# Neighbourhood attention with woven projections: low weight halves by adding DMAs, and low-rank follow-ups queued later

## The chip, the cores and the metric

The kernel runs on one core of a Trainium2 chip. The metric is the device time of one execution in microseconds. A core has a matrix engine (PE, with its weight loads shown as PEld), three elementwise engines (DVE, ACT, POOL), a queue engine that issues most transfers (SP), and 16 DMA engines that move the data. Each engine works through its own instruction queue in order and waits at semaphores for the others.

## The reference, cut to what matters

One layer of a hybrid backbone: a modulated RMS norm, one wide input projection `h @ w_in`, an RWKV branch and a neighbourhood-attention branch side by side, a gated merge, and a feed-forward part. There are 640 tokens (512 latent grid tokens and 128 context tokens), 1024 features, 8 heads of 64 in each branch, all in float32.

```python
h = _rmsnorm(x, p["norm1_g"]) * (1.0 + sc1) + sh1
u_rw, u_na, gate_rw, gate_na = jnp.split(h @ p["w_in"], IN_SPLITS, axis=-1)
o_rw, s_new = _rwkv_branch(u_rw, s0, ...)      # u_rw: r, k, v, and the low-rank inputs wd, ad, gd
q, k, v = jnp.split(u_na, 3, axis=-1)
o_na = _na_latent(q, k, v, ctx_k, ctx_v, p["na_rpb"])
merged = (jax.nn.sigmoid(gate_rw) * (o_rw @ p["w_o_rwkv"])
          + jax.nn.sigmoid(gate_na) * (o_na @ p["w_o_na"]))
x = x + g1 * (merged @ p["w_out"])
```

In the RWKV branch `wd` goes through a tanh and `gd` through a sigmoid before they are multiplied by their second, low-rank matrices (`rw_w_up`, `rw_a_up`, `rw_g_up`); every column of `u_rw` is first mixed with its left and right neighbour in time (`_centred_shift`).

## The kernel before, in words

**Products in halves.** A float32 product of full precision is made of three faster ones: each operand is a high half (a cast to the short form) and a low half (what the cast lost), and PE computes high*high + high*low + low*high. `feat_gen` issues them for one 128-column chunk of weights: 16 matmuls that use the weight's high half `whi`, then 8 that use its low half `wlo`, for the token half 0 to 319, and the same 24 for the tokens 320 to 639. One chunk is thus a **unit** of 48 matmuls.

**Making the halves.** `wdma` (L163) has SP load a chunk of 512 KB into a staging buffer `wst`; there are two such buffers. `wcast` makes the halves, in one of two ways, chosen by one letter of the string `wl` for each unit. With "d": ACT casts `wst` to `whi` (L173) and DVE subtracts, `wlo = wst - whi` (L175). With "p": ACT writes `-wst` in the short form to `wlo` (L171), POOL issues a DMA that adds `wst` to it (L172), and ACT casts `whi` (L173). In the "p" form the staging buffer is free for the next load when the adding DMA has landed, in the "d" form when DVE has subtracted.

**The stage around the change.** Neighbourhood attention runs in 20 blocks (4 pairs of heads, five query blocks each) in the loop over `k` with 22 steps. Step `k` issues `na_o(k-2)` (PE: weighted values; ACT L185 and DVE L186 split the result), `na_l(k)` (PE L899: logits into a PSUM tile `lg` of which there is one; DVE L905 or L912: bias and maximum), `na_t(k-1)` (PE L928: transposes of the probabilities `L` into PSUM tiles `pt`, two of them; ACT L933 copies them out), the exponentials (ACT L909 or L914), 6 woven matmuls, `na_m(k)` (DVE L921: reciprocals; POOL L922: `L` times the reciprocal, two for the two heads), then a bias window for a later block (`window`, POOL L801) and, at step 7 alone, `prep_cast` (ACT L570 casts the second low-rank matrices, POOL L573 makes their low halves), then some 12 more woven matmuls, and at some steps two rounds of the modulation product (`ada_gen`, PE L984, with the loads L965 on SP). From step 10 on the preparation of the first RWKV head pair (`prep_a`, `prep_b`) is interleaved too; its low-rank products (PE L592, L594) borrow the `pt` tiles and ACT L597 or L600 reads them out; its products for the key norm end in DVE L629 and L631.

**The woven units.** The woven matmuls are those of nine units, in the order of `order`: l0 l1 k0 r0 v0 l2 g0 g1 g2 (low-rank inputs, keys, receptances, values, gates). `stream` gives one matmul at a time, loads two units ahead, and queues the cast of unit i+1 when unit i has made 6 matmuls.

**The queue of follow-ups.** `later(fn, cost, more)` appends work with a due time of `off[0] + more` woven matmuls, where `off[0]` is 6 in this stage; the cast of the next unit is appended as due at once. `tick` counts down one per matmul and issues from the head of the list only: what stands behind an entry that isn't due waits for it, even if it is due itself.

```python
    def tick(n):
        for p in pend:
            p[0] -= n
        while pend and pend[0][0] <= (-24 if hold[0] else 0):
            pend.pop(0)[2]()
```

After a unit's last matmul `proj_gen` queues the copy out of PSUM, and the neighbour mixing (`shift`: ACT L521, DVE L522 and L524) in two parts. For the low-rank units `lora_gen` adds a tanh (ACT L711 for l0; L706 and DVE L707 for l2), and for l0 and l1 two calls of `two` that split a result (ACT L701, DVE L702 into `LX`).

**What sets the order.** In this stage `tc.manual_schedule(engines=FIRST)` keeps PE, POOL, DVE and ACT in exactly the order in which the Python code issues. SP isn't among them: its queue is ordered by the planner, which expects times by a model of its own.

Of the kernel before, what the change touches and what calls it, by code (L numbers as in the profile page):

```python
# [7 lines left out]
F32 = mybir.dt.float32  # L8
F32R = mybir.dt.float32r
AF = mybir.ActivationFunctionType  # L10
ALU = mybir.AluOpType
# [59 lines left out]
    h2=0.91, jobs=((2, 9, 28), (2, 9, 28), (2, 9, 28), (2, 11, 28)),  # L71
    mds=((4, 12), (4, 12), (4, 12), (4, 14)), bud=((1.8, 0.8), (1.3, 1.8)), off=6, tk=2, h3=1,
    h4=1.07, g1=2, km="dddddddd", kb="ddpd", ma="d", yo="pppp", r0="pd", rl=(0, 0, 0), lh=(0, 0, 1, 1),
    wl="dddddddddppppppppppppppppppppppppppdpppppppppppp", nu=9, jo=(2, 0, 1), na=(
        "6.0.12.0.1 6.0.12.0.0 6.0.12.0.0 6.0.12.0.2 6.0.12.0.0 6.0.12.0.2 6.0.12.0.0 6.0.12.0.2 6.0.12.0.0 "
        "6.0.12.0.2 6.0.12.1.0 6.1.12.1.2 6.2.12.2.0 6.1.12.2.2 6.0.12.2.0 6.1.12.1.2 6.2.14.2.0 "
        "6.2.14.1.2 6.2.14.2.0 6.2.14.2.0 6.3.18.2.0 10.0.10.0.0"))
# [30 lines left out]
def body(ctx: ExitStack, tc: tile.TileContext, xs, xp, cols, consts, w_ada, b_row, w_rw, w_qkv,  # L108
# [3 lines left out]
    pe, act, dve, pool, sp = nc.tensor, nc.scalar, nc.vector, nc.gpsimd, nc.sync  # L112
# [22 lines left out]
    def nm(s):  # L135
        cn[0] += 1
        return f"{s}_{cn[0]}"
# [28 lines left out]
    def wcast(w, eng=None):  # L166
        st, n, pl, nhl = w
        hi = pl.tile([P, 1024], F32R, tag="whi", bufs=nhl, name=nm("whi"))
        lo = pl.tile([P, 1024], F32R, tag="wlo", bufs=nhl, name=nm("wlo"))
        if eng is pool:  # L170
            act.activation(lo[:, :n], st[:, :n], AF.Copy, scale=-1.0)  # L171
            pool.dma_start(lo[:, :n].bitcast(F32), st[:, :n], accum_op=ALU.add)  # L172
        act.copy(hi[:, :n], st[:, :n])  # L173
        if eng is not pool:
            dve.tensor_tensor(out=lo[:, :n], in0=st[:, :n], in1=hi[:, :n].bitcast(F32), op=ALU.subtract)  # L175
        return hi, lo

    def wload(src, eng=None):
        return wcast(wdma(src), eng)
# [269 lines left out]
    lg_ = kp.tile([P, NT], F32, name="lg_")  # L449
# [28 lines left out]
    def later(fn, cost=(0.5, 0), more=0):  # L478
        if off[0]:
            pend.append([off[0] + more, cost, fn])  # L480
        else:
            fn()
# [21 lines left out]
    def proj_gen(ci, out, ps_, usb, utag, ubufs, w):  # L504
        U = usb.tile([P, 643], F32, tag=utag, bufs=ubufs, name=nm("U"))
        pool.memset(V(U[:, :], [[513, 2]]), 0.0)
        pool.memset(U[:, 642:643], 0.0)
        ps0 = ps_()
        yield from feat_gen(ps0, w, (hh, hl), 8, 0, H2)
        later(lambda: act.copy(U[:, 1:321], ps0[:, :H2]))  # L510
        ps1 = ps_()
        yield from feat_gen(ps1, w, (hh, hl), 8, H2, NT)

        def u_out():
            act.copy(U[:, 321:513], ps1[:, 0:192])
            act.copy(U[:, 514:642], ps1[:, 192:320])

        def shift(a, b, u):
            o = out[:, a:b]
            n = b - a  # L520
            act.activation(o, U[:, u:u + n], AF.Identity, scale=dcol(dm, ci))  # L521
            dve.scalar_tensor_tensor(out=o, in0=U[:, u - 1:u - 1 + n], scalar=col("mu0", ci),  # L522
                                     in1=o, op0=ALU.mult, op1=ALU.add)
            dve.scalar_tensor_tensor(out=o, in0=U[:, u + 1:u + 1 + n], scalar=col("mu1", ci),  # L524
                                     in1=o, op0=ALU.mult, op1=ALU.add)

        later(u_out, (0.6, 0))
        later(lambda: shift(512, 640, 514), (0.4, 0.7), 2)
        later(lambda: shift(0, 512, 1), (0.8, 1.5), 5)
# [163 lines left out]
    gtag = ["fl"]  # L693

    def lora_gen(i, w):

        yield from proj_gen(12 + i, lg_, flps, sb, "U", len(gtag), w)

        def two(d):
            rr, ro = slice(64 * d, 64 * d + 64), slice(64 - 64 * d, 128 - 64 * d)  # L700
            act.copy(LX[i][d][rr, :], lg_[rr, :])  # L701
            dve.tensor_tensor(out=LX[i][d][ro, :], in0=lg_[rr, :], in1=LX[i][d][rr, :].bitcast(F32),  # L702
                              op=ALU.subtract)

        if i == 2:
            later(lambda: act.activation(lg_, lg_, AF.Tanh, scale=0.5), (0.8, 0), 8)  # L706
            later(lambda: dve.tensor_scalar(out=lg_, in0=lg_, scalar1=0.5, scalar2=0.5, op0=ALU.mult, op1=ALU.add),  # L707
                  (0, 0.5), 12)
            return
        if i == 0:  # L710
            later(lambda: act.activation(lg_, lg_, AF.Tanh), (0.8, 0), 8)  # L711
        for d in range(2):
            later(lambda d=d: two(d), (0.8, 0.8), 12 + 6 * d)

    def some(n):
        for _ in range(n):
# [3 lines left out]
    def unit(g, e):  # L720

        i, eng = int(g[1:]), eng_of(e)
        if g[0] in "ab":
            return 24 if g[0] == "a" else 18, lambda: merge_load(g[0], i), \
                lambda wt: merge_cast(*wt, eng), lambda w: merge_gen(g[0], i, w)
        if g[0] == "g":
            return 48, lambda: wdma(w_rw[15 + i]), lambda w: wcast(w, eng), \
                lambda w: gate_gen(i, w, flps, sb, gtag[-1])
        ci, dst = {"k": (4 + i, kt_), "r": (i, rt_), "v": (8 + i, vp0), "l": (12 + i, lg_)}[g[0]]
        return 48, lambda: wdma(w_rw[ci]), lambda w: wcast(w, eng), \  # L730
            lambda w: proj_gen(ci, dst, flps, sb, "U", len(gtag), w) if g[0] != "l" else lora_gen(i, w)
# [48 lines left out]
    with s1:  # L780
# [93 lines left out]
        with ExitStack() as s1b:  # L874
# [127 lines left out]
            with tc.manual_schedule(engines=FIRST):  # L1002
                for k, step in enumerate(PRM["na"].split()):
                    a, p, b, q, n = (int(x) for x in step.split("."))
# [994 lines left out]
```

## Time and profile before

| | us |
|---|---|
| median of three runs | 1191.83 (1191.1 to 1192.4) |
| the profiled execution | 1191.72 |
| its span, first to last instruction | 1189.7 |
| PE busy in the span | 1124.1 (94%) |
| DVE, ACT, POOL busy | 777.5, 530.5, 205.1 |
| mean granted clock of PE | 0.985 |

The stage of the change lies between 120 and 258 us from the start of the span. In the stretches 120 to 160, 160 to 200 and 200 to 240 us PE is busy for 39.04, 38.57 and 36.12 of 40 us each; DVE for 22.52, 20.21 and 22.30; ACT for 26.25, 22.73 and 24.33; the DMA engines have a share of 0.70, 0.79 and 0.51.

In a row of a timeline the first number is the start in us, the second the time from the start to the end of the run of like instructions, then engine, line, operation, output and inputs, and how many; square brackets give idle time just before and what ended it. A matmul of 320 columns is shown with 309 ns, but they overlap in the pipeline: ten of them fill about 1.55 us. In a table by stretches the columns are the length, busy time and count of PE, PEld, DVE, ACT and POOL, the granted clock, the DMA share and GB/s. In a table of groups the numbers behind the bar are busy time in us, mean ns of one, idle time before.

### The profile page before, as it was taken

How to read it: one execution, taken by the hardware profiler on the slowest of the kernel's cores; microseconds unless marked ns; L12 is line 12 of the kernel's file. 1: busy time of each engine (PE TensorE's matmuls, PEld its weight loads, DVE VectorE, ACT ScalarE, POOL GpSimd, SP SyncE). 2: the span in 40 equal slices, each digit the busy share in tenths (PEclk: the TensorE clock that was granted, in tenths of full speed). 3: DMA queues.
4: the chain of work that ended last, by engine and by line, in shares of the span. 5: the costliest groups of instructions: out<-in, count | busy, mean ns of one | idle time of the engine just before them, and what ended most of it. 6: DMA issues, size and time to landing. Idle time of an engine off the chain costs nothing.

```text
span 1189.7 us, 26921 instructions
## 1 busy us (share of the span) xinstructions
PE 1124.1 (94%) x11160; PEld 998.3 (84%) x11160; DVE 777.5 (65%) x1630; ACT 530.5 (45%) x1053; POOL 205.1 (17%) x273
## 2 busy tenths in 40 slices
PE   6999999999999999999599799989999999999998
PEld 4688877789888988888488678889899989998997
DVE  4564455559469658836474675888568757775675
ACT  4444666554564664565133342654224422442340
POOL 1162244320111211111101250100001000000000
PEclk9999999999999999999799999999999999999999
DMA  9762767553333514433654851312312231232122
GB/s 335 265 117 84 244 216 230 191 146 98 103 93 84 153 50 104 123 93 79 200 138 110 245 218 54 107 49 79 104 57 86 89 107 54 89 100 90 59 75 103
DMA packets 61906, 149.42 MB, mean 126 GB/s; under 512 B 7732, under 2 KB 23732, under 8 KB 61784
## 3 DMA queue, kind: packets, MB, share of 16 engines
q1 hardware_dynamic: 55592, 131.56, 33.6%
q0 software_dynamic: 5328, 14.94, 6.8%
q8 instruction: 88, 1.44, 0.5%
q10 hardware_dynamic: 864, 1.20, 0.3%
q14 instruction: 34, 0.28, 0.1%
HBM read 118.41 MB, written 14.32 MB: 112 GB/s over the span
## 4 chain that ended last, share of the span: by engine, by line
PE 65%; DVE 8%; ACT 3%; DMA 2%; issue 1%; SPq 0%; ACTq 0%; DVEq 0%; POOLq 0%
PE f L1718 23%; PE acc L284 17%; PE fl L197 13%; DMA wlo<-wst 1%; DVE pr L1250 1%; PE w L1324 1%; PE w L1351 1%; DVE RL L1254 1%; PE mm L197 1%; PE w L1364 1%; PE w L1336 1%; PE w L1148 1%; DMA o<-o_d 1%; PE w L1196 1%; PE w L1126 1%
## 5 line engine op out<-in xcount | busy, mean ns | idle before, releaser
L1718 PE MATMUL f<-t,whi 128*128 128x320 f32 x640 | 141.4, 309 | 0.0
L1718 PE MATMUL f<-b,whi 128*128 128x320 f32 x608 | 136.5, 312 | 3.6 <-ACT b L185 1.8
L284 PE MATMUL acc<-whi,u 128*128 128x512 f32 (+1 forms) x448 | 136.0, 385 | 0.0
L197 PE MATMUL fl<-h,whi 128*128 128x320 f32 x704 | 126.5, 319 | 0.8 <-issue 0.8
L197 PEld LDWEIGHTS fl<-h,whi 128*128 128x128 f32 x704 | 106.1, 188 | 5.6 <-issue 0.9
L173 ACT CAST whi<-wst 128x1024 fp32r<-128x1024 f32 (+2 forms) x86 | 81.5, 953 | 64.7 <-PE acc L284 32.5
L1718 PEld LDWEIGHTS f<-t,whi 128*128 128x128 f32 x640 | 107.1, 188 | 0.0
L1718 PEld LDWEIGHTS f<-b,whi 128*128 128x128 f32 x608 | 103.0, 190 | 4.8 <-ACT b L185 2.2
L1718 PE MATMUL f<-t,wlo 128*128 128x320 f32 x320 | 98.9, 309 | 0.0
L284 PEld LDWEIGHTS acc<-whi,u 128*128 128x128 f32 x448 | 83.5, 188 | 16.7
L1718 PE MATMUL f<-b,wlo 128*128 128x320 f32 x304 | 94.7, 312 | 1.4 <-DVE wlo L1762 1.4
L1759 ACT CAST whi<-ws 128x1024 fp32r<-128x1024 f32 x40 | 42.0, 1051 | 108.7 <-PE f L1718 48.5
L1773 POOL TENSOR_TENSOR ws<-wst 128x512 f32<-128x512 f32 x20 | 28.2, 1409 | 341.3 <-DVE wlo L1762 226.7
L175 DVE TENSOR_TENSOR wlo<-wst,whi 128x1024 fp32r<-128x1024 f32 (+1 forms) x49 | 62.0, 1274 | 37.2 <-ACT whi L173 36.6
L284 PE MATMUL acc<-wlo,u 128*128 128x512 f32 (+1 forms) x224 | 86.3, 385 | 0.0
L284 PE MATMUL acc<-whi,h 128*128 128x512 f32 x240 | 78.0, 399 | 1.2 <-DVE h L398 1.1
L172 POOL DMA_DIRECT2D wlo<-wst x37 | 32.6, 881 | 232.4 <-ACT wlo L171 212.9
L1558 DVE SCALAR_TENSOR_TENSOR tt<-acc,G 128x512 f32<-128x512 f32 (+1 forms) x51 | 34.7, 681 | 50.5 <-PE acc L284 50.5
L197 PE MATMUL fl<-h,wlo 128*128 128x320 f32 x352 | 66.5, 321 | 0.0
L197 PE MATMUL fl<-o,whi 128*128 128x320 f32 x224 | 46.3, 337 | 16.8 <-DMA o<-o_d 10.0
L1759 ACT CAST whi<-wst 128x1024 fp32r<-128x1024 f32 (+1 forms) x48 | 41.3, 869 | 42.3 <-PE acc L284 37.6
L1718 PEld LDWEIGHTS f<-t,wlo 128*128 128x128 f32 x320 | 60.1, 188 | 0.0
(333 smaller groups left out, 2539.1 us busy)
## 6 DMA issues: line engine op xcount, KB each, us to landing
wst<-in_w_dram SPq DMA_DIRECT2D x66, 512.0 KB
wst<-in_w_rw_dram SPq DMA_DIRECT2D x31, 512.0 KB
wa<-in_w_ada_dram SPq DMA_DIRECT2D x24, 512.0 KB
wlo<-wst POOLq DMA_DIRECT2D x22, 512.0 KB, 4.5
f<-in_w_ada_dram SPq DMA_DIRECT2D x16, 512.0 KB
wst<-in_w_qkv_dram SPq DMA_DIRECT2D x12, 512.0 KB
o<-o_d SPq DMA_DIRECT2D x14, 320.0 KB
x<-in_xs_dram SPq DMA_DIRECT2D x8, 512.0 KB
```

Of the source, the lines that this page charges most:

```text
L172: pool.dma_start(lo[:, :n].bitcast(F32), st[:, :n], accum_op=ALU.add)
L173: act.copy(hi[:, :n], st[:, :n])
L175: dve.tensor_tensor(out=lo[:, :n], in0=st[:, :n], in1=hi[:, :n].bitcast(F32), op=ALU.subtract)
L197: pe.matmul(ps[:, :t1 - t0], w[:, a:a + 128], x[:, k0 + kt, t0:t1], start=n == 0, stop=n == 3 * nk - 1)
L284: pe.matmul(pss[i][:, a:b], lhs(x, kt, ts_), w[:, cs_], start=ki == 0 and n == 0, stop=ki == last and n == 2)
L1126: pe.matmul(t[r0:r0 + 32, 64 * i:64 * i + 64], S.BK[l // 10][own, l % 10, 0, 32 * bk:32 * bk + 32], V(AG[own, l, h, :], [[0, 2], [1, 32]], ...
L1148: pe.matmul(pr[h][hrows[h ^ i], o_], x[hrows[h], :], R_[hrows[h], l, :], start=True, stop=True)
L1196: pe.matmul(pt[h][hrows[h ^ i], o_], S.BK[l // 10][hrows[h], l % 10, i, :], idh(h), start=True, stop=True)
L1558: dve.scalar_tensor_tensor(out=tt, in0=ps[:, a:b], scalar=c, in1=G[:, g, sl], op0=ALU.mult, op1=ALU.mult)
L1718: pe.matmul(ps[:, :H2], w_[:, c_], x_[:, kt, :], start=first and kt + n == 0, stop=last and kt == 3 and n == 2, skip_group_check=more)
L1759: act.copy(r[0][:, :width], src())
L1773: eng_x(PRM["se"][i - 1]).tensor_tensor(out=o_, in0=x, in1=y, op=op)
```

## The change

The first part lets seven units that used "d" use "p": k0, r0, v0, l2, g0, g1 and g2. The second part, in `wcast`, puts the adding DMA of a "p" unit into the queue of follow-ups with a due time of 6 + 4 matmuls, wherever two PSUM tags are in use (that is in this stage), in place of issuing it between the two ACT instructions; this holds for the unit k1 too, which is cast at the end of the stage and had "p" already. The third part makes the follow-ups of the low-rank units due later: the tanh at 6 + 15 matmuls after the unit's end in place of 6 + 8, the split or the final scaling at 6 + 20 in place of 6 + 12, the second split again 6 later.

```diff
-    wl="dddddddddppppppppppppppppppppppppppdpppppppppppp", nu=9, jo=(2, 0, 1), na=(
+    wl="ddpppppppppppppppppppppppppppppppppdpppppppppppp", nu=9, jo=(2, 0, 1), na=(
...
         if eng is pool:
             act.activation(lo[:, :n], st[:, :n], AF.Copy, scale=-1.0)
-            pool.dma_start(lo[:, :n].bitcast(F32), st[:, :n], accum_op=ALU.add)
+            add = lambda: pool.dma_start(lo[:, :n].bitcast(F32), st[:, :n], accum_op=ALU.add)
+            later(add, (0, 0), 4) if len(gtag) > 1 else add()
         act.copy(hi[:, :n], st[:, :n])
...
         if i == 2:
-            later(lambda: act.activation(lg_, lg_, AF.Tanh, scale=0.5), (0.8, 0), 8)
+            later(lambda: act.activation(lg_, lg_, AF.Tanh, scale=0.5), (0.8, 0), 15)
             later(lambda: dve.tensor_scalar(out=lg_, in0=lg_, scalar1=0.5, scalar2=0.5, op0=ALU.mult, op1=ALU.add),
-                  (0, 0.5), 12)
+                  (0, 0.5), 20)
             return
         if i == 0:
-            later(lambda: act.activation(lg_, lg_, AF.Tanh), (0.8, 0), 8)
+            later(lambda: act.activation(lg_, lg_, AF.Tanh), (0.8, 0), 15)
         for d in range(2):
-            later(lambda d=d: two(d), (0.8, 0.8), 12 + 6 * d)
+            later(lambda d=d: two(d), (0.8, 0.8), 20 + 6 * d)
```

## The prediction

> **What bounds the kernel now.** I read the page first, then who PE waits for inside the stage, then the timelines of PE, DVE, ACT and POOL around each of those waits. All numbers are us from the start of the span.
>
> ```profile
> span 1189.7 us, 26921 instructions
> PE 1124.1 (94%) x11160; PEld 998.3 (84%) x11160; DVE 777.5 (65%) x1630; ACT 530.5 (45%) x1053; POOL 205.1 (17%) x273
> ```
>
> PE is the bound almost everywhere, so the change can win only what PE idles in its stage, and lose what it makes PE idle. PE's waits between 115 and 255, in total, times, longest:
>
> ```profile
> PE pt L928 <- POOL L L922: 3.2, 4, 1.2
> PE pt L928 <- ACT pre L600: 2.4, 1, 2.4
> PE pt L928 <- DVE kk L629: 1.5, 1, 1.5
> PE lg L899 <- ACT L L914: 0.3, 1, 0.3
> ```
>
> That is 7.4 us in all: the ceiling of the direct gain. The clock is a second, indirect one:
>
> ```profile
> 225.80:229.20 3.40, 1.51 (x11) 1.43 (x12) 2.54 (x6) 3.35 (x7) 0.00 (x0) 1.00 0.20 76
> 229.20:232.60 3.40, 3.40 (x15) 3.40 (x14) 2.42 (x6) 1.74 (x5) 1.92 (x3) 0.50 0.60 204
> ```
>
> After a stretch of 3.4 us with PE busy for 1.51 the granted clock is 0.50 for the next 3.4 us.
>
> **Part one: DVE is relieved, ACT, POOL and the DMA engines are loaded.**
>
> ```profile
> L175 DVE TENSOR_TENSOR wlo<-wst,whi 128x1024 fp32r<-128x1024 f32 x8 | 10.9, 1360 | 5.8 <-ACT whi L173 5.7
> ```
> ```profile
> L171 ACT ACTIVATE wlo<-wst 128x1024 fp32r<-128x1024 f32 x16 | 16.8, 1052 | 0.1
> ```
> ```profile
> L172 POOL DMA_DIRECT2D wlo<-wst x37 | 32.6, 881 | 232.4 <-ACT wlo L171 212.9
> ```
>
> Seven units: DVE loses 7 x 1.36 = 9.5, ACT gains 7 x 1.05 = 7.4, POOL 7 x 0.88 = 6.2, and seven transfers of 512 KB join. None of this is on PE's path as such: each engine idles a third of the stage or more. What counts is what stands behind these instructions at PE's waits. I worked out the order on each engine before and after by following the queue of follow-ups with its rule that only the head is issued, counting woven matmuls from l0's first.
>
> **The waits at 160 and 162.** Rows of PE, DVE and POOL:
>
> ```profile
> 160.21 0.55 PE L928 MATMUL pt<-K,L 128*128 128x128 f32 x3 [0.77 <-POOL L L922]
> 161.97 0.55 PE L928 MATMUL pt<-K,L 128*128 128x128 f32 x3 [1.22 <-POOL L L922]
> 162.28 1.72 PE L197 MATMUL mm<-h,whi 128*128 128x320 f32 x10
> ...
> 171.67 0.46 PE L197 MATMUL mm<-h,wlo 128*128 128x320 f32 x2
> ```
> ```profile
> 157.56 0.82 DVE L702 TENSOR_TENSOR lx<-lg__618,lx 64x640 fp32r<-64x640 f32 x1 [1.84 <-ACT lx L701]
> 158.39 0.22 DVE L921 RECIPROCAL m<-m 128x1 f32<-128x1 f32 x2
> ```
> ```profile
> 158.72 3.20 POOL L922 TENSOR_TENSOR L<-L,m 128x384 f32<-128x384 f32 x2 [5.43 <-DVE m L921]
> ...
> 164.01 1.61 POOL L922 TENSOR_TENSOR L<-L,m 128x384 f32<-128x384 f32 x2 [1.35 <-DVE m L921]
> 165.58 0.78 POOL L801 TENSOR_TENSOR bm<-win,nam 128x256 f32<-128x256 f32 x1
> 166.31 1.53 POOL L573 TENSOR_TENSOR UL<-upw,uh 64x256 fp32r<-64x256 f32 x2
> ```
>
> The reciprocals of block 6 stand behind l1's first split (L702) in DVE's queue, and POOL's two multiplications take 3.20 in place of 1.61 while DVE subtracts. The new due times put that split at matmul 122, behind these reciprocals (114), and r0's subtraction is gone. What ACT now does earlier (k0's extra 1.05, moved from matmul 72 to 80) makes block 6's exponentials about 1.6 later than before by my chain, but without the split in front the multiplications end near 159.5, where PE wants the second at 159.1. I take 1.8 of the 1.99 as won (bounds 0.9 to 2.0), and the 0.3 of L914 too, since the splits and the cast leave the place in front of block 4's exponentials. **Gain 2.1.**
>
> The same delay makes r0 tight. Its cast moves from matmul 120 to 128 and its adding DMA is due at 138. In POOL's queue that is behind block 7's multiplications (132), the window and `prep_cast` at step 7. The exponentials of that chain, from first to last:
>
> ```profile
> 162.93 0.62 ACT L909 ACTIVATE L<-L,m 128x384 f32<-128x384 f32 x1
> ...
> 164.05 0.19 ACT L909 ACTIVATION_READ_ACCUMULATOR L<-L,m 128x1 f32 x1
> ```
>
> After the change PE ends block 6's transposes at 162.3 - 2.1 = 160.2. ACT copies them out, and block 7's exponentials, 1.3 long (162.93 to 164.24), start near 161.2 and end at 162.5. Then l1's second split: the cast on ACT, taken as long as DVE's row, and 0.82 on DVE, to 164.1; only then, in DVE's queue, the reciprocals, 0.1. POOL: multiplications 1.61 to 165.8, window 0.78 to 166.6, L573 1.53 to 168.1. So the DMA starts at 168.1. Its landing times, in the stretch nearest to this stage (246 to 300), and of all 37 in the span:
>
> ```profile
> DMA to landing us min/median/max: 4.4/5.9/6.4
> ```
> ```profile
> DMA to landing us min/median/max: 2.9/4.5/8.5
> ```
>
> With 5.9 the low half is there at 174.0. PE wants it at 171.67 - 2.1 = 169.6, so it **waits 4.4** (at 4.4: 2.9; at 8.5, the longest of any add in the trace, of a smaller transfer: 7.0). I take the median of the stretch because the DMA engines are as busy here:
>
> ```profile
> 172.00:174.00 2.00, 2.00 (x24) 1.65 (x24) 1.80 (x3) 2.00 (x5) 1.45 (x2) 1.00 0.94 373
> ```
>
> The Trainium skill (DMA: Bandwidth & Descriptors, "Anatomy of one DMA") fits such a DMA as 2.0 us plus bytes over 436 GB/s, 3.2 us for 512 KB as an estimate; by it PE would wait 1.7 and the whole sum would be 2.7 better; but the five landings here are all above 4.4.
>
> A wait of 4.4 leaves one stretch of 3.4 us with PE busy for less than 1.51, so the clock falls to half for 3.4 us once more. I charge what the stretch at 229 cost (below): **1.4 lost** (0 to 1.7).
>
> **The wait at 207.**
>
> ```profile
> 205.51 1.22 DVE L175 TENSOR_TENSOR wlo<-wst,whi 128x1024 fp32r<-128x1024 f32 x1
> 206.65 0.74 DVE L629 SCALAR_TENSOR_TENSOR kk<-kt__620,C,pt 128x512 f32<-128x512 f32 x1
> ```
> ```profile
> 207.53 0.85 PE L928 MATMUL pt<-K,L 128*128 128x128 f32 x6 [1.51 <-DVE kk L629]
> ```
>
> g0's subtraction goes, L629 starts 206.65 - 205.51 = 1.14 earlier: **gain 1.1** (0 to 1.5). ACT's extra 1.05 lies in idle time before its next piece, L185.
>
> **The wait at 227 and the clock after it.**
>
> ```profile
> 225.45 0.74 ACT L706 ACTIVATE lg__618<-lg__618 128x640 f32<-128x640 f32 x1 [2.00 <-DVE lg__618 L524]
> 226.09 1.03 ACT L173 CAST whi<-wst 128x1024 fp32r<-128x1024 f32 x1
> 227.03 0.94 ACT L600 ACTIVATE pre<-pt,D 128x320 f32<-128x320 f32 x2
> ```
> ```profile
> 227.69 0.94 PE L928 MATMUL pt<-K,L 128*128 128x128 f32 x6 [2.38 <-ACT pre L600]
> 228.39 0.83 PE L197 MATMUL mm<-h,wlo 128*128 128x320 f32 x4
> 229.06 4.04 PE L197 MATMUL mm<-h,whi 128*128 128x320 f32 x16
> ```
>
> PE waits for `pt` tiles that L600 empties. L600 (issued at matmul 308) stands behind l2's tanh (302) and g1's cast (306). With the new due times they come at 309 and 314, behind it, so L600 follows its products at once: **gain 2.4** (0.7 if another ACT instruction slips in). Then no stretch is half idle here and the half clock goes: sixteen matmuls took 4.04, while the ten at 162.28 took 1.72 with the last 0.31 long, so they start (1.72 - 0.31)/9 = 0.157 apart and 16 take 2.66: **gain 1.4** (0 to 1.7). g1's halves are then late by 8 matmuls and an ACT instruction, but g1 begins at 336.
>
> **The end of the stage.** The 1.2 left of L922's 3.2 lie at block 19:
>
> ```profile
> 246.69 0.33 PE L928 MATMUL pt<-K,L 128*128 128x128 f32 x1 [0.57 <-POOL L L922]
> ```
> g2's subtraction (1.36 by its group's mean) goes from DVE's queue in front of block 19's maximum, while ACT's extra 1.05 there is ahead of the split only: **gain 1.1** (0 to 1.2).
>
> **Sum.** -2.1 + 4.4 + 1.4 - 1.1 - 2.4 - 1.4 - 1.1 = -2.3, against a profiled execution of 1191.7 (span 1189.7 and 2.0 around it), 0.1 under the median. For edges I add 0.3: k0's first matmul finds its high half ready only some 0.5 ahead, and SP's loads wait for landings in place of subtractions (the buffer of r0 is free at 174 in place of 161), which the modulation loads behind them can feel. So 1191.8 - 2.0 = **1189.8**. The bounds of the terms give this case a range of its own of 1186.5 to 1194.5.
>
> **The rivals.**
>
> *r0's low half is in time.* If DVE and ACT run ahead of my chain by some 4 us (POOL reaches the DMA by 164), neither the wait nor its clock loss comes: 1189.8 - 5.8 = 1184.0. For it: my chain has eight links, each of which I could place too late. Against: POOL has L573 at 166.31 even before, with no extra work in front. Chance 0.15.
>
> *The clock stays up after r0's wait.* Two adjacent stretches could share the idle time. Then 1189.8 - 1.4 = 1188.4. The row with 1.51 busy speaks against it. The Trainium skill (TensorE: Matmul & The Clock Gate, "What's actually happening") has the clock fall after at least one idle window of about 3.4 us in windows that run freely; read as a window idle throughout, it would give this result. By the row at 225.80 half a window is enough. Chance 0.15.
>
> *The adds land slowly, and the kernel is slower.* Place: the DMA engines between 144 and 176, where they are nearly full. If an add takes 10.5 in place of 5.9, r0's wait is 9.0, and k0 waits too. Its add is due 22 matmuls before its low half, as r0's is (138 and 160), and those 22, with the step's other work between them, lie between 162.28 + 12 x 0.157 = 164.2 and 171.67 for r0: 7.5 us, so 3.0 more. That makes 1189.8 + 4.6 + 3.0 = 1197.4, with SP's loads later too. It eats the gains from a landing of about 7.7 on, and passes 0.2% near 9. For it: the share of 0.94 at 172, and 1.04 where k0's add would run:
>
> ```profile
> 146.00:148.00 2.00, 1.70 (x22) 1.28 (x20) 0.85 (x6) 1.41 (x6) 0.73 (x2) 1.00 1.04 408
> ```
>
> Against: 6.4 is the longest of the five. Chance 0.20.
>
> *Nothing comes of it.* The four queues are fixed by hand, and a wait taken away in one place comes back one block on: the preparation's products follow PE closely there. Gains and losses stay under 1 us: 1191.8. Chance 0.10.
>
> **How the numbers follow.** The forecast has 0.40. What can be told from no change is 0.2%, 2.4 us, so faster begins at 1189.4. The forecast's own range puts 0.17 there, the early low half 0.15, the clock that stays up 0.12: faster 0.44. Slower, above 1194.2: 0.18 of the slow adds and 0.04 of the forecast: 0.22. The rest, 0.34, is the same. The range leaves out the far half of the early and of the slow case: 1185.0 to 1195.5.
>
> **What would show it.** Right: PE's first matmul with r0's low half behind an idle time of 3 to 6 that a DMA ended, a half clock right behind it and none near 229; no wait of L928 for L922 near 160, for L600, or over 0.5 for L629; L629 right behind L524. Wrong: L573 before 164; landings in the stage under 4 or over 8; PE waiting in L984 for loads; k0's first matmuls waiting for ACT.

## The result and the profile after

The changed kernel takes 1199.39 us (median of 7 runs, 1195.25 to 1201.22) against 1193.51 for the kernel before in the same measurement. The ratio on record, taken over these runs, is 1.0055, with a 95% interval of 1.0039 to 1.0070; the quotient of the two medians is 1.0049. It is slower, where a slightly faster one was forecast, and lies above the range (1195.5). The profiled execution took 1198.61, with this on its page:

```profile
span 1196.8 us, 26937 instructions
PE 1130.8 (94%) x11160; PEld 1001.7 (84%) x11160; DVE 770.0 (64%) x1623; ACT 536.6 (45%) x1060; POOL 211.7 (18%) x280
```

DVE lost 7.5 us and ACT and POOL gained 6.1 and 6.6 (9.5, 7.4 and 6.2 were worked out). The span of the profiled executions grew by 7.1, the median by 5.9: the profiled execution of the kernel before, 1191.72, is one of its shorter ones. PE's waits between 115 and 270 us, in total, times, longest, in the changed kernel (all line numbers behind L172 are one higher than before):

```profile
PE pt L929 <- POOL L L923: 3.7, 2, 2.3
PE mm L198 <- DMA wlo<-wst: 2.7, 1, 2.7
PE psa L985 <- DMA wa<-in_w_ada_dram: 2.0, 1, 2.0
PE po L947 <- DVE on L187: 1.2, 1, 1.2
PE pt L929 <- DVE kk L630: 0.5, 1, 0.5
PE psa L985 <- DMA f<-in_w_ada_dram: 0.2, 1, 0.2
```

The 7.4 us of waits that the prediction listed have become 10.3 us, and they are others. PE's timeline of the changed kernel shows where each of them stands:

```profile
159.35 1.71 PE L198 MATMUL mm<-h,whi 128*128 128x320 f32 x10
...
165.26 1.05 PE L985 MATMUL psa<-wa,cs 128*32 128x512 f32 x4 [2.03 <-DMA wa<-in_w_ada_dram]
166.48 1.05 PE L985 MATMUL psa<-f,cs 128*32 128x512 f32 x4 [0.17 <-DMA f<-in_w_ada_dram]
...
175.01 0.90 PE L198 MATMUL mm<-h,wlo 128*128 128x320 f32 x2 [2.67 <-DMA wlo<-wst]
...
212.78 0.84 PE L929 MATMUL pt<-K,L 128*128 128x128 f32 x6 [0.47 <-DVE kk L630]
...
230.50 0.88 PE L929 MATMUL pt<-K,L 128*128 128x128 f32 x6
...
237.39 0.66 PE L947 MATMUL po<-PT,vs 128*64 128x128 f32 x8 [1.23 <-DVE on L187]
...
241.53 0.55 PE L929 MATMUL pt<-K,L 128*128 128x128 f32 x3 [2.27 <-POOL L L923]
243.49 0.90 PE L929 MATMUL pt<-K,L 128*128 128x128 f32 x3 [1.42 <-POOL L L923]
```

Four of these rows have their twin in the prediction: the ten matmuls that started at 162.28 now start at 159.35 (2.9 earlier), r0's first low-half matmuls at 175.01 in place of 171.67 (3.3 later), the transposes of 207.53 at 212.78 (5.3 later) and those of 227.69 at 230.50 (2.8 later). So the early gain was made, was lost between 160 and 183, came back by half at 207 and 227, and was lost again between 231 and 250. The granted clock, in stretches (the number third from the end), shows that each loss has a half clock (0.50) in it, behind the wait:

```profile
171.60:175.00 3.40, 0.75 (x6) 0.48 (x4) 2.43 (x5) 3.37 (x8) 2.86 (x4) 0.93 0.84 171
175.00:178.40 3.40, 3.39 (x20) 2.50 (x21) 1.09 (x3) 0.50 (x2) 0.36 (x1) 0.50 0.83 123
178.40:181.80 3.40, 3.40 (x17) 3.40 (x16) 0.66 (x4) 2.09 (x7) 0.98 (x3) 0.57 0.84 223
...
239.90:243.30 3.40, 0.55 (x3) 0.31 (x3) 3.37 (x6) 2.44 (x4) 2.80 (x2) 0.92 0.13 48
243.30:246.70 3.40, 3.21 (x13) 3.21 (x14) 2.12 (x9) 3.20 (x10) 1.91 (x5) 0.50 0.60 120
246.70:250.10 3.40, 3.40 (x20) 3.07 (x20) 1.73 (x2) 3.17 (x5) 2.23 (x3) 0.57 0.57 117
```

**Who is late, and why.** SP's queue shows it. First the kernel before, around g0's subtraction (which ends at 206.73; `wst` is a staging buffer, `wa` and `f` are modulation loads, `o_d` are the stores of the attention's output `on`):

```profile
206.75 0.33 SPq L163 DMA_DIRECT2D wst<-in_w_rw_dram  x1
...
216.70 0.33 SPq L965 DMA_DIRECT2D wa<-in_w_ada_dram  x1
...
218.51 1.20 SPq L953 DMA_DIRECT2D o_d<-on  x2
```

The same in the changed kernel, with the early part ahead of it:

```profile
152.35 0.36 SPq L163 DMA_DIRECT2D wst<-in_w_rw_dram  x1
...
156.33 0.59 SPq L966 DMA_DIRECT2D wa<-in_w_ada_dram  x1
...
224.07 0.33 SPq L163 DMA_DIRECT2D wst<-in_w_rw_dram  x1
224.50 0.39 SPq L966 DMA_DIRECT2D wa<-in_w_ada_dram  x1
...
225.92 0.67 SPq L966 DMA_DIRECT2D f<-in_w_ada_dram  x1
226.64 1.10 SPq L954 DMA_DIRECT2D o_d<-on  x2
```

L163 at 206.75 and 224.07 is the load of g2's weights, which needs g0's staging buffer. With the adding DMA that buffer is free only when the add has landed, and the add itself was issued late, so the load leaves 17 us later. Behind it in SP's queue stand four modulation loads of 512 KB and then the two stores `o_d` (L954) of a finished head pair. All of them leave within 3 us, the stores last, 2.8 us after DVE has written the last of their data (223.81). The stores read the tiles `on`, of which there is one set; until they are out, ACT can't write the next pair's first block:

```profile
235.04 0.38 ACT L186 CAST on<-po 128x128 fp32r<-128x128 f32 x1 [5.45 <-DMA o_d<-on]
```

ACT stands for 5.45 us with the exponentials behind this cast, DVE and POOL behind ACT, and PE at 237 to 243 behind them. In the early part v0's load leaves at 152.35 (145.78 before), when k0's add has landed. The modulation load that PE then waits 2.03 for follows at 156.33. That is only 0.5 later than before (155.84), but PE wants it 2.8 earlier, and v0's load now moves just ahead of it. The stores of the first head pair move there too, and ACT stands for them as it does at 235; block 7's exponentials follow at 163.41, where the prediction had them near 161.2:

```profile
161.39 0.39 ACT L186 CAST on<-po 128x128 fp32r<-128x128 f32 x1 [3.90 <-DMA o_d<-on]
...
163.41 0.61 ACT L910 ACTIVATE L<-L,m 128x384 f32<-128x384 f32 x1 [0.94 <-DVE m L906]
```

All eight kernels here in which k0 is made by an add have this wait (2.1 to 4.0 us near 162); the six in which k0 is subtracted have none. r0's add stands at the end of the chain behind these exponentials. POOL's timeline of the changed kernel has the issues of the adds of k0, r0 and g0:

```profile
147.53 1.04 POOL L172 DMA_DIRECT2D wlo<-wst  x1
...
170.44 0.88 POOL L172 DMA_DIRECT2D wlo<-wst  x1
...
217.75 0.89 POOL L172 DMA_DIRECT2D wlo<-wst  x1
```

From here to the released load or matmul (152.35, 175.01, 224.07) are 4.8, 4.6 and 6.3 us. These adds land about as fast as forecast (5.9); of the seven issued between 140 and 250 us the slowest, v0's at 174.49, took 7.7, and PE waited for r0's alone. What is late is what stands behind their landing.

### The profile page after: what moved, and what is told of

Its sections match the earlier page's. It is cut to its first block, busy times and chain, and to the rows that moved or that the text cites. A ratio compares the mean times of both kernels' runs of the same rounds, so it can differ in the third digit from the quotient of the medians.

```text
span 1196.8 us, 26937 instructions
## 1 busy us (share of the span) xinstructions
PE 1130.8 (94%) x11160; PEld 1001.7 (84%) x11160; DVE 770.0 (64%) x1623; ACT 536.6 (45%) x1060; POOL 211.7 (18%) x280
## 4 chain that ended last, share of the span: by engine, by line
PE 70%; DVE 14%; DMA 7%; ACT 4%; issue 3%; POOL 1%; SPq 0%; DVEq 0%; ACTq 0%; POOLq 0%
PE acc L285 22%; PE f L1719 21%; PE fl L198 9%; PE mm L198 4%; DMA wa<-in_w_ada_dram 2%; DVE pr L1251 2%; DVE RL L1255 1%; DMA o_d<-on 1%; DVE Rt L1285 1%; DVE AG L1158 1%; PE pt L929 1%; PE lg L900 1%; PE w L1352 1%; DVE TG L1161 1%; PE po L947 1%
## 5 line engine op out<-in xcount | busy, mean ns | idle before, releaser
L172 POOL DMA_DIRECT2D wlo<-wst x44 | 38.9, 884 | 236.6 <-ACT wlo L171 216.9
L176 DVE TENSOR_TENSOR wlo<-wst,whi 128x1024 fp32r<-128x1024 f32 (+1 forms) x42 | 52.9, 1269 | 33.8 <-ACT whi L174 33.3
```

The costliest lines, as they stand in the source:

```text
L172: add = lambda: pool.dma_start(lo[:, :n].bitcast(F32), st[:, :n], accum_op=ALU.add)
```

## The experiments

Theory A: the staging buffers, freed by landings and not by subtractions, hold up SP's queue, and the modulation loads and stores in it come late. Theory B: the later due times do the harm. Theory C: ACT's extra work and the extra DMA traffic do it as such. Each run is given as a ratio to the kernel before, with its 95% interval.

**One part alone.** `e_due` is the kernel before with the third part of the diff (the due times) only; `e_dma` is the changed kernel without that part. The edit of `e_due`, which `e_dma` reverses:

```diff
-            later(lambda: act.activation(lg_, lg_, AF.Tanh, scale=0.5), (0.8, 0), 8)
+            later(lambda: act.activation(lg_, lg_, AF.Tanh, scale=0.5), (0.8, 0), 15)
...
-            later(lambda d=d: two(d), (0.8, 0.8), 12 + 6 * d)
+            later(lambda d=d: two(d), (0.8, 0.8), 20 + 6 * d)
```

> Only the later due times of the low-rank follow-ups; all seven units keep the subtraction on DVE, and the adding DMA of k1 is issued at once as in the kernel before. Theory A (the loss comes from staging buffers that become free only when an add has landed, so that weight loads are late, bunch with other loads and hold up what stands behind them in SP's queue): faster than the kernel before by 3 to 6 us; the waits of PE at 160 and 227 and the half clock near 229 are gone, no wait of PE for a DMA in the stage, no wait of ACT for the store of the attention output. Rival B (the later due times are the fault, since they push casts and adds back): slower than before by 2 us or more. Rival C (the extra ACT work and DMA traffic as such are the fault): like A here.

> The adding DMAs for the seven units, queued 10 matmuls late as in the changed kernel, but the old due times of the low-rank follow-ups. Theory A: slower than before by 3 to 8 us; SP waits for landings in front of weight loads for 20 us or more in total, PE waits for modulation weights or the store of the attention output holds up ACT; the wait at 227 stays and grows by the extra 1.05 of ACT. Rival B: within 1.5 us of the kernel before, r0's low half in time. Rival C: slower by 3 us or more, without long waits of SP for landings.

`e_due`: 0.9991 (0.9982 to 1.0001); `e_dma`: 1.0020 (1.0009 to 1.0030). Theory B falls: the due times alone cost nothing. They gain next to nothing either, where theory A had expected 3 to 6 us, and the reason was news. The wait at 227 for L600 is gone in `e_due`, but ACT then stands in its place:

```profile
226.81 0.39 ACT L185 CAST on<-po 128x128 fp32r<-128x128 f32 x1 [2.09 <-DMA o_d<-on]
```

PE's wait at 227 had covered the stores: without it PE waits 1.0 and 1.4 at 234 and 236, behind ACT. `e_dma`, slower by less than theory A's 3 to 8 us, shows the reverse: its stores are issued at 226.51, as late as in the changed kernel, but PE waits 3.32 for L601 at 234.25 first, and the cast comes just when they are out:

```profile
234.84 0.38 ACT L186 CAST on<-po 128x128 fp32r<-128x128 f32 x1 [0.31 <-DMA o_d<-on]
```

With the two parts together the stores are late and their cover is gone: 1.0055, more than 0.9991 and 1.0020 add up to.

**The queueing of the adds, and POOL's order.** `e_now` issues each add at once; `e_pc` moves `prep_cast` out of the way of r0's add.

```diff
-            later(add, (0, 0), 4) if len(gtag) > 1 else add()
+            add()
```
```diff
-                    if k == 7:
+                    if k == 5:
```

> The changed kernel, but each adding DMA is issued at once between the two ACT instructions, in place of 10 matmuls later. Theory A: staging buffers come free some 3 us earlier per unit, so it is faster than the changed kernel by 3 to 6 us (1193 to 1197 where that has 1199.4); SP's waits for landings fall to about half of 27 us, r0's low half costs PE less than 1 us. Rival B and rival C: within 1.5 us of the changed kernel.

> The changed kernel, but the cast of the second low-rank matrices with its POOL part (prep_cast) is issued at step 5 in place of step 7, so that r0's add no longer stands behind it in POOL's queue. Theory A: r0's add starts some 1.5 us earlier, PE's wait for r0's low half falls from 2.7 to about 1.2 and its half clock may go: faster than the changed kernel by 1.5 to 4 us; the wait for modulation weights near 165 (2.0) and ACT's wait for the store near 235 (5.4) stay. If r0's add is the whole loss, it is as fast as the kernel before.

`e_now`: 0.9995 (0.9981 to 1.0008), 0.6% better than the changed kernel; of the waits near 240 none over 0.25 is left, while PE still waits 1.9 for r0's low half (under 1 was expected) and 3.2 for modulation loads. Theory C falls with it: ACT's work and the traffic are the same, and only the moment of the adds differs. `e_pc`: 1.0058 (1.0046 to 1.0071), a miss; r0's wait stays at 2.6. Its add left at 171.05, no earlier than in the changed kernel (170.44), since the multiplications ahead of it in POOL's queue came 2.1 later. So this run doesn't tell what the place of `prep_cast` is worth.

**The stores, and g0's buffer.** `e_oact` issues the stores from ACT's queue; `e_g0d` gives g0 its subtraction back.

```diff
-                        sp.dma_start(t_d[ft], t.bitcast(F32))
+                        act.dma_start(t_d[ft], t.bitcast(F32))
```
```diff
-    wl="ddppppppppppppppppppppppppppppppppdpppppppppppp"
+    wl="ddppppdpppppppppppppppppppppppppppdpppppppppppp"
```

> The changed kernel with the stores of the attention's split outputs (o_d, L954) issued from ACT's queue in place of SP's. Theory A (the stores stand in SP's queue behind g2's weight load, which waits for the landing of g0's adding DMA at 224, so that the buffers `on` come free late): the stores are issued by 221, ACT's wait for them at L186 (5.4 in the changed kernel) falls under 0.5, PE's waits at 237 to 243 (1.2 for L187, 2.3 and 1.4 for L923) go, and with them the half clock at 243: 1199.4 - 4.9 - about 1.7 = 1192 to 1194. Rival (the stores are late beside another delay, that of POOL's multiplications): no change, 1198 to 1200. Rival C (ACT pays for issuing, with waits for DVE's half): the wait goes, others on ACT come, 1196 to 1199.

> The changed kernel with g0 alone back on ACT's cast and DVE's subtraction. Theory A: g0's staging buffer is free at about 208 and not at 224, g2's load and the stores behind it in SP's queue go out some 10 us earlier, and the waits of PE at 237 to 243 go with the half clock after them: 1192 to 1195, while the wait for L630 at 212 grows from 0.5 to at most 1.5. Rival (the wait at 241 comes from the later follow-ups or from DVE's queue, not from SP): 1198 to 1200.

`e_oact`: 1.0006 (0.9989 to 1.0023); its median, 1194.2 us, is just above theory A's range. Its stores leave 0.02 us behind the last cast, and the next block's cast waits for PE only:

```profile
227.74 0.27 ACT L186 CAST on<-po 128x128 fp32r<-128x128 f32 x1 [1.72 <-PE po L947]
228.03 0.81 ACTq L954 DMA_DIRECT2D o_d<-on  x2
...
234.27 0.38 ACT L186 CAST on<-po 128x128 fp32r<-128x128 f32 x1 [0.16 <-PE po L947]
```

g2's load is no earlier in this run (228.41), so it is the stores' place behind it, and not the late load, that cost the waits of 4.9 and the half clock after them. The Trainium skill (DMA: Bandwidth & Descriptors, "Issuing engines are not separate DMA queues") says that transfers share the 16 DMA engines whoever starts them, and that a second issuing engine saves only the time to issue. No run here speaks against the sharing; but by the second half this edit would be worth little, and it was worth 5 us, since what it saved was a place in a queue that waits in order.

`e_g0d`: 1.0018 (1.0009 to 1.0027), just above the range of theory A, and well away from its rival. g2's load leaves at 214.49, the stores at 225.78, as soon as their data are there (225.83), and the wait for L630 is back at 1.61. Half of the late loss was regained: ACT no longer waits for these stores (the cast at 234.00 waits for PE), and of L923's wait 1.42 is left at 241.

**r0 and k0.** `e_r0d` gives only r0 its subtraction back. `e_krd` gives it to k0 and r0, with the adds still queued; `e_now2` is the same with the adds issued at once, as in `e_now`. The edit of the string for these two; `e_r0d` has "ddpdpp" in front:

```diff
-    wl="ddppppppppppppppppppppppppppppppppdpppppppppppp"
+    wl="ddddppppppppppppppppppppppppppppppdpppppppppppp"
```

> The changed kernel with r0 alone back on the subtraction. Theory A: r0's first low-half matmul waits for nothing (2.7 in the changed kernel), l2's load goes out before 168 and not at 175, and the half clock at 175 goes: 1199.4 - 2.7 - 1.7 = 1195, less if the modulation loads behind l2's also come in time (down to 1192.5). Rival (the early loss is the bunch of loads behind k0's landing at 152, so PE's wait of 2.0 for a modulation load at 165 stays, and the half clock with it): 1196.5 to 1198. The late waits near 240 stay in both.

> The changed kernel with k0 and r0 back on the subtraction and the adding DMAs still queued ten matmuls later. Theory A (what counts is when the staging buffers come free; ten matmuls and what stands ahead in the queue are some 5 us): g0's add is issued near 212 and lands near 218 (204.6 when issued at once), g2's load and the stores behind it stay late, ACT waits for the stores and PE in L923 near 238: 1193 to 1197, 5 to 8 above the version that issues at once. Rival (only k0 and r0 were short of time, the queueing costs nothing): 1188 to 1190.

> The changed kernel with the adding DMAs issued at once and k0 and r0 back on the subtraction; v0, l2, g0, g1 and g2 by adding DMAs, and the later due times. Theory A: the early part runs as before without its waits at 160 and 162, and v0 to g2 have the time their landings need, so the gains at 207 and 227 are kept: 1189.5 to 1191.5, faster than the kernel before by 0.2 to 0.3%. Rival (any adding DMA in this stage frees its buffer late enough to hurt the modulation loads and the stores): 1193 to 1196, PE waiting again in L985 or for the stores.

`e_r0d`: 1.0038 (1.0025 to 1.0050), close to its rival (1196.5 to 1198): r0's wait and the half clock at 175 go, the wait of 1.9 for a modulation load at 165 stays, a second one of 2.2 comes at 220, and the waits near 240 stay. In `e_krd`, where k0 subtracts too, the wait at 165 is 0.45, so most of it comes with k0's add. The load PE waits for leaves at the same moment in both (156.31 and 156.33 in the changed kernel); but without the add v0's load is out of its way 3.7 earlier (148.67), the DMA engines are less busy when PE wants it (a share of 0.58 from 164 to 168, 0.91 in the changed kernel), and PE itself comes 1.3 later.

`e_krd`: 1.0009 (0.9994 to 1.0023). `e_now2`: **0.9960 (0.9946 to 0.9974)**, 1188.3 us (median of 6 runs) beside 1193.47: faster than both kernels. The two differ in the code by the ten matmuls of queueing alone. In `e_krd`, SP and then PE:

```profile
218.31 0.33 SPq L163 DMA_DIRECT2D wst<-in_w_rw_dram  x1
...
220.15 0.59 SPq L966 DMA_DIRECT2D f<-in_w_ada_dram  x1
220.79 0.95 SPq L954 DMA_DIRECT2D o_d<-on  x2
```
```profile
231.35 0.66 PE L947 MATMUL po<-PT,vs 128*64 128x128 f32 x8 [1.07 <-DVE on L187]
...
235.49 0.55 PE L929 MATMUL pt<-K,L 128*128 128x128 f32 x3 [2.27 <-POOL L L923]
237.45 0.90 PE L929 MATMUL pt<-K,L 128*128 128x128 f32 x3 [1.42 <-POOL L L923]
```

The same three waits as in the changed kernel, with a half clock behind them, though nothing early went wrong. In `e_now2`, SP and then ACT:

```profile
214.79 0.33 SPq L163 DMA_DIRECT2D wst<-in_w_rw_dram  x1
...
219.28 0.33 SPq L966 DMA_DIRECT2D f<-in_w_ada_dram  x1
219.97 0.81 SPq L954 DMA_DIRECT2D o_d<-on  x2
```
```profile
226.22 0.39 ACT L186 CAST on<-po 128x128 fp32r<-128x128 f32 x1 [0.16 <-PE po L947]
```

The load leaves 3.5 us earlier, the five loads are spread over 4.5 us (to 219.28) and not packed into 1.8 (to 220.15 in `e_krd`), and the stores are out in time. PE waits 0.8 for two modulation loads near 217; its next output product stands 2.5 later for it than in `e_krd` (219.17 and 216.69). No stretch of this stage has a lowered clock.

Over most of these runs and the three below, PE's waits between 230 and 245 go with ACT's wait for the stores. There are none over 0.3 in `e_now`, `e_oact`, `e_now2` and `e_k0p`, where ACT doesn't wait for the stores; 2.4 us in `e_due` (ACT 2.09), 2.2 in `e_g02` (1.75), 3.8 in `e_r0d` (3.55), 4.8 in `e_krd` (6.47) and 4.9 in the changed kernel (5.45). Four runs don't tell: in `e_g0d` (1.4) and `e_pc` (5.0) the trace names PE as what ACT waited for, and in `e_dma` and `e_n2o` PE waits 3.3 for L601 first.

**What makes the best version.** `e_n2o` is `e_now2` with the old due times; `e_g02` is `e_now2` with adds for g0 and g2 only; `e_k0p` is `e_now2` with k0 by an add as well. The edits of the last two, against `e_now2`:

```diff
-    wl="ddddppppppppppppppppppppppppppppppdpppppppppppp"
+    wl="ddddddpdppppppppppppppppppppppppppdpppppppppppp"
```
```diff
-    wl="ddddppppppppppppppppppppppppppppppdpppppppppppp"
+    wl="ddpdppppppppppppppppppppppppppppppdpppppppppppp"
```

> The version with k0 and r0 by subtraction and the adding DMAs issued at once, with the old due times of the low-rank follow-ups. If the later due times bring what the prediction gave them: PE's wait of 2.4 for L601 near 226 and the half clock after it come back (2.4 + 1.4), and the wait for L923 near 160 in part: 1191 to 1193. Rival (ACT's order near 226 differs anyway once the subtractions are gone, so the due times are worth little): 1188 to 1189.5.

> The version with the later due times and adding DMAs issued at once, used for g0 and g2 alone; k0, r0, v0, l2 and g1 by subtraction. If the gain comes only from the subtractions in front of L630 and of block 19's maximum and from the due times, and the adds of v0, l2 and g1 only delay loads: 1186.5 to 1188.5, as good as with them or better. Rival (DVE's relief in v0, l2 and g1 counts too): 1189.5 to 1192.

> The best version so far (k0 and r0 by subtraction, adding DMAs issued at once, later due times) with k0 too by an adding DMA. It prices the landing of k0's low half alone, where the prediction put 0.3 with the other edges. Theory A: v0's load goes out at about 151 in place of 148.8, bunched with the modulation loads behind it, and PE waits 1 to 2 for a modulation load near 166; no low half is waited for: 1189.5 to 1191, 1.2 to 2.5 over the version without it. Rival 1 (issued at once it lands early enough): no difference, 1187.5 to 1189. Rival 2 (the loads of l2 and g0 behind it are carried along, to the stores near 220): 1192 to 1194.

`e_n2o`: 1.0022 (1.0007 to 1.0037), worse than expected: the waits for L601 (3.3) and for L923 at 160 and 162 (2.0) are back, and one for L598 (1.9) comes that the kernel before doesn't have. The due times are worth 0.6% here, though alone on the kernel before they were worth nothing that can be told. `e_g02`: 0.9991 (0.9976 to 1.0005); its rival was right that the adds of v0, l2 and g1 carry part of the gain. In its trace ACT stands 1.75 for the stores at 227, and POOL's work comes late at 234 and 236 (0.83 and 1.42), as in `e_due`. Why those three matter was not separated further.

`e_k0p`: 1.0002 (0.9987 to 1.0017). The trace has the wait that theory A expected:

```profile
165.87 1.36 PE L985 MATMUL psa<-wa,cs 128*32 128x512 f32 x4 [1.99 <-DMA wa<-in_w_ada_dram]
```

with a lowered clock behind it (0.70 and 0.79 in the next two stretches of 3.4 us). The time is dearer than the trace: the profiled spans of `e_k0p` and `e_now2` lie 2.2 apart (1188.8 and 1186.6), the medians 5.6, which is in the range of rival 2 and not of theory A. But the stores that rival 2 names (they leave at 222.04) hold nobody up in this trace. Its 12 runs spread from 1188.5 to 1197.0, and the profiled one, 1190.6, is among the shortest. By the ratios k0's add costs 0.4%, by the two profiled executions 0.2%; by what chain the longer runs lose more is open, since only one execution is profiled.

## Why the prediction was wrong

- *The waits at 160 and 162, gain 2.1.* Right: both are gone, and the ten matmuls behind them start 2.9 earlier, of which 0.4 is an earlier start of the whole stage.
- *The wait at 207, gain 1.1.* Right: 0.47 of 1.51 is left.
- *The wait at 227 and its half clock, gains 2.4 and 1.4.* The wait is gone as forecast. That it covered the stores of the attention's output was not seen: the prediction said where the stall came from, but not what would be late next. `e_due` and `e_dma` show it: with the stores out in time `e_due` still has 2.09 of the 5.45 that ACT stands in the changed kernel.
- *The end of the stage, gain 1.1.* Right: no wait of block 19 is left in the list.
- *r0's low half, loss 4.4.* Right in mechanism, and in the order of the chain: the add is issued at 170.44 (168.1 was worked out) and lands after 4.6, not 5.9. Of the 2.3 between, 2.2 are there when block 7's exponentials start (163.41), behind ACT's wait for the first stores, which the chain didn't have. PE came 2.7 later than worked out (172.34 in place of 169.6), so it waited 2.67.
- *The half clock after it, loss 1.4.* It lasts two stretches and not one. The first low-half matmul was 3.3 later than before; the modulation's matmuls behind it are 6.3 later (first row of the two fences below). So 2.9.
- *Edges, loss 0.3.* **This is the step that failed.** It named the mechanism (SP's loads wait for landings, and the modulation loads stand behind them) and gave it a price near nothing without following the queue, and it left out the stores, which stand in the same queue. Measured: 2.2 of waits for the modulation loads at 165, 4.9 for the stores at 237 to 243, and 2.5 for the half clock after those: the low-half matmuls right behind the waits are 6.9 later than before, the next block's products 9.4 (second and third row).

PE's timeline of the kernel before, and then of the changed one:

```profile
176.73 0.62 PE L984 MATMUL psa<-wa,cs 128*32 128x512 f32 x2
...
237.17 1.42 PE L197 MATMUL mm<-h,wlo 128*128 128x320 f32 x8
...
240.28 0.66 PE L946 MATMUL po<-PT,vs 128*64 128x128 f32 x8
```
```profile
183.01 0.62 PE L985 MATMUL psa<-wa,cs 128*32 128x512 f32 x2
...
244.04 2.48 PE L198 MATMUL mm<-h,wlo 128*128 128x320 f32 x8
...
249.66 0.66 PE L947 MATMUL po<-PT,vs 128*64 128x128 f32 x8
```

The sum with these in place: -2.3 as forecast without edges, less 1.7 at r0, plus 2.2, 1.5, 4.9 and 2.5, is +7.1, the growth of the span. That it closes to the tenth is luck. Followed row by row, the changed kernel stands at -2.9 against the one before at the ten matmuls, at +0.5 behind the modulation product (167.47 beside 166.95), at +3.3 and +6.3 around the half clock, at +5.3, +2.8 and +1.2 (234.24 beside 233.03) as the gains come in, at +6.9 and +9.4 around the second half clock, at +7.9 behind block 19 (255.62 beside 247.72) and at +7.1 at the end. So the early gain was 0.8 more than forecast; the modulation loads cost 3.4 and not 2.2, since a late load also keeps the matmuls of `wa` and `f` from alternating; and 0.8 came back behind the stage.

Of the rivals, the slower one named slow landings; k0's and r0's landed in 4.8 and 4.6, so its mechanism was not the one; that its time (1197.4) was the nearest is luck. Its half sentence "with SP's loads later too" needed no slow landing. The rival of a clock that stays up was wrong: the stretch with 0.75 of 3.4 us busy is followed by half clock. The Trainium skill (TensorE: Matmul & The Clock Gate, "What's actually happening") asks for an idle window of about 3.4 us; here, as in the row with 1.51 before, a stretch that is partly busy suffices: PE's idle time at r0 is 2.67.

## What to carry to other kernels

When an operation is moved to a DMA, ask when its source buffer comes free and read the queue that waits for that buffer to its end: every load and store behind the waiting one moves with it, those of other parts of the kernel too. Issue such a DMA as early as its data allow, give it to the tiles whose successors are loaded with slack, and keep stores that free a single buffer out of a queue that waits for landings. Before counting a removed wait as a gain, look for what it covered: here taking away 3.8 us laid bare a store, and undoing that part alone made the changed kernel faster, while in `e_now2`, whose stores leave in time, the same part is worth 0.6%.

## What the runs showed of the hardware

The half clock came as one stretch of 3.4 us behind the stretch with 1.51 us of PE busy in the kernel before, and as two, 6.8 us, behind those with 0.75 and 0.55 in the changed kernel. The length of the wait alone doesn't settle whether it comes: the wait of 2.03 at 165 in the changed kernel had no lowered clock behind it, the one of 1.99 in `e_k0p` had. Where it comes, a wait costs more than its length: the 2.67 us at r0 were followed by a loss of 2.9, the 4.9 us near 240 by one of 2.5.

The modulation matmuls of `wa` and `f` overlap when they alternate: sixteen of them took from 165.09 to 166.95 in the kernel before, 1.9 us. In the changed kernel, where `f` came after `wa`, the last eight took from 165.26 to 167.47, 2.2 us with a wait of 0.17 in it.

In a burst of transfers the last was late: in the changed kernel the stores of 2 x 320 KB, issued at 226.64 behind five loads of 512 KB that had left since 224.07, held `on` until 235.04, 8.4 us; in `e_krd`, likewise behind five loads, until 230.04, 9.2 us. In `e_oact`, issued from ACT at 228.03 just ahead of the same five loads, they held it for at most 6.2.
